# Places of matmul operands within 128-byte blocks of the on-chip memory, in a two-block hybrid layer

## The chip, the cores and the metric

The kernel runs on one core of a Trainium2 chip. The metric is the device time of one execution in microseconds (us). It is taken several times, and the median counts.

## The reference

Two model blocks run one after the other on 256 tokens of width 1024, all in float32. The first is a modulated RMS norm, a mixer of three small attentions with gates, and a convolution FFN; the second is gated linear attention, then dilated window attention. Cut to the large products:

```python
h = _rmsnorm(x, g0) * (1.0 + sc1) + sh1
z = h @ w_in                                   # 1024 -> 2248 + 3 * 1024
merged = sum(sigmoid(zg[i] + b[i]) * (y[i] @ w_branch[i]) for i in range(3))
x = x + g1 * _rmsnorm(merged @ w_out, g)
h = _rmsnorm(x, g2) * (1.0 + sc2) + sh2
a, g = split(h @ w_up, 2)                      # 1024 -> 2 * 2816
x = x + g2 * _rmsnorm((gelu(conv3(a)) * g) @ w_down, g3)
# second block: y = gla_mixer(x);  x = layer_norm(alpha * x + y)
#               y = dilated_mixer(x, shared_kv(x));  x = layer_norm(alpha * x + y)
```

## The kernel before, in words

Each float32 operand of a large product is split into a high part, rounded to the float32r type, and a low part, the remainder, in the same type. A product then takes three matmuls (`mm3`, L267): low part of the standing operand against the high part of the moving one, high against low, high against high. The class `Stream` (L100) brings the weights in one after the other: a DMA of 1 MB into a tile `raw`, then for each 1024 columns a copy on ScalarE to the tile `whi` (L154) and a subtraction on VectorE to the tile `wlo` (L155). There are six buffers of each.

The large products come in two forms. In `wstat` (L512, called by `wpair`) a 128 x 128 piece of the weights is loaded into TensorE and stands still there, while 256 columns (the tokens) of the transposed activations move through. In `tokmm` the activations are loaded 128 x 128 at a time, and 512 columns of the weights move. Every matmul has its own load, which runs while the matmul before it moves its columns. The keys of the weights of the first form are `in1`, `inc`, `zg`, `br`, `up`, `gla`, `gk`, `kvk` and `sq`; the others (`out`, `dn`, `gvg`, `gout`, `kvv`, `sout`) move.

The transposed activations of a stage are a pair of tiles (high, low) made by `big8` (L393), which use two buffers in turn: `hhi`, `hlo` for the first projections and the gates; `mhi`, `mlo` for the merged branches; `h2hi`, `h2lo` for the FFN; `x2hi`, `x2lo` for gated linear attention; `x3hi`, `x3lo` for window attention. `yhi`, `ylo` are the outputs of the three attentions.

The class `Lines` (L203) rounds every tile in the pools up to a multiple of 128 bytes, so each operand of the large products begins on a multiple of 128 bytes in each partition. A column of weights in a slice is 4 bytes, a loaded slice 512 bytes, and a moved slice 1024 or 2048 bytes.

Of the kernel before, what the change touches and what calls it, by code (L numbers as in the profile page):

```python
# [8 lines left out]
F32 = mybir.dt.float32  # L9
F32R = mybir.dt.float32r  # L10
# [8 lines left out]
S = 256  # L19
D = 1024  # L20
KK = 8
# [9 lines left out]
ORD3 = "u00 u01 c0 w00 w01 r0 n00 n01 u10 u11 c1 w10 w11 r1 N10 N11"  # L31
ORD4 = "u00 u01 c0 w00 w01 r0 u10 o00 u11 c1 o01 w10 r1 w11 o10 o11"
SC_SWA = float(128.0 ** -0.5)

COLS = {}

# [63 lines left out]
class Stream:  # L100
# [31 lines left out]
    def _chunk(self, i):  # L132
        nc = self.nc
        key, ap, n, part = self.items[i]
        if part < 0:
            raw = self.early.tile([128, n], F32, tag="early", name="early", bufs=3)
        else:
            raw = self._raw()
        if not part:
            for o in range(0, n, 1024):  # L140
                nc.sync.dma_start(raw[:, o:o + 1024], ap[:, o:o + 1024])
            self.done.append(raw)
            return
        nc.sync.dma_start(raw[:, :n], ap)
        parts = []
        for o in range(0, n, part) if part > 0 else range(0, -part, 1024):
            m = min(part, n - o) if part > 0 else min(1024, -part - o)
            hi = self.pool.tile([128, 1024], F32R, tag="whi", name="whi", bufs=self.hlbufs)
            lo = self.pool.tile([128, 1024], F32R, tag="wlo", name="wlo", bufs=self.hlbufs)
            with ExitStack() as st:  # L150
                for ins in self.behind:
                    st.enter_context(self.tc.issue_after(ins))
                st.enter_context(self.tc.high_priority(self.pri))
                i0 = nc.scalar.activation(hi[:, :m], raw[:, o:o + m], AF.Copy)  # L154
                i1 = nc.vector.tensor_sub(lo[:, :m], raw[:, o:o + m], hi[:, :m].bitcast(F32))  # L155
                self.last = (i0.ins, i1.ins)
            parts.append((hi, lo))
        self.done.append((part, parts) if part > 0 else (raw, (1024, parts)))
# [68 lines left out]
def hybrid_blocks(ctx, tc, A, out, dbg=None):  # L227
# [3 lines left out]
    cn = Lines(ctx.enter_context(tc.tile_pool(name="cn", bufs=1)), sm)  # L231
# [3 lines left out]
    def open_pool(name):  # L235
        st = ExitStack()
        p = st.enter_context(tc.tile_pool(name=name, bufs=1))
        return Lines(p, st.enter_context(tc.tile_pool(name=name + "s", bufs=1))), st.close

    p1a, close_p1a = open_pool("p1a")  # L240
    p0, close_p0 = open_pool("p0")
# [5 lines left out]
    def mm_t():  # L247
        return ps.tile([128, 512], F32, tag="mm", name="mm", bufs=2)
# [4 lines left out]
    def dump(name, t):  # L253
        if dbg and name in dbg:
            nc.gpsimd.dma_start(dbg[name], t)

    def mm(o, l, r, start, stop, share=False):
        return pe.matmul(o, l, r, start=start, stop=stop, skip_group_check=share)  # L258
# [126 lines left out]
    for h in range(4):  # L385
        sq = p0.tile([128, 2, S], F32, name="sq0", tag="sq0", bufs=2)
# [3 lines left out]
        for b in range(2):  # L390
            mm(pr[:, 256 + b:257 + b], ssq[:, b * 128:(b + 1) * 128], ones[:, 0:1], h == 0 and b == 0, h == 3, True)

    def big8(dt, name):  # L393
        return cn.tile([128, KK, S], dt, name=name, tag="big8r", bufs=2)

    hT = (big8(F32R, "hhi"), big8(F32R, "hlo"))
    qk = [acc_t(), acc_t()]
    vps = [mm_t(), mm_t()]
# [83 lines left out]
    pr = at_t()  # L482
    for b in range(2):
        mm(pr[:, b * 128:(b + 1) * 128], r1[:, b:b + 1].to_broadcast([128, 128]), ident, True, True)
    rbc = cn.tile([128, S], F32, name="rbc")
    dve.tensor_copy(rbc, pr[:, 0:S])
    h32, at = first_h(0, ga)
    for j in range(KK):
# [28 lines left out]
    def wpair(key, a, fresh=False):  # L517


        w = ws.get(key)  # L520
        p = mm_t()
        if fresh:
            for n in range(2):
                o = p[:, n * 256:(n + 1) * 256]
                W = [wsl(w, n * 1024 + k * 128, n * 1024 + (k + 1) * 128) for k in range(KK)]
                for k, l in enumerate(W):
                    mm(o, l[1], a[0][:, k, :], k == 0, False)
                    mm(o, l[0], a[0][:, k, :], False, False)
                for k, l in enumerate(W):
                    mm(o, l[0], a[1][:, k, :], False, k == KK - 1)  # L530
            return p
        for n in range(2):
            wstat(p[:, n * 256:(n + 1) * 256], w, n * 1024, a)
        return p
# [29 lines left out]
    p = wpair(("inc", 0), hT)  # L564
# [206 lines left out]
    for i in range(2):  # L771
        w = ws.get(("br", i))
        for u in range(4):
            n = 4 * i + u
            p = mm_t()
# [6 lines left out]
        if i:  # L782
            w2 = ws.get(("br", 2))
            branch2(0)
            branch2(1)
        gates(9 + 2 * i)
    mT = (big8(F32R, "mhi"), big8(F32R, "mlo"))
    for i in range(4):
        if i > 1:
# [118 lines left out]

    rms_residual(y, xn, mod[0], x1, ORD1, (xr, mod[2]))
    dump("x1", x1)  # L910
    h2 = (big8(F32R, "h2hi"), big8(F32R, "h2lo"))

    def ev_h2(j, p, act, dve):
        for low in range(2):
# [76 lines left out]
    for i in range(4):  # L991
        p = wpair(("gk", i), x2T)
        if i < 2:
            act.activation(qT[:, 2 * i:2 * i + 2, :], p, AF.Copy, scale=SC_SWA)
        else:
# [190 lines left out]
    xqt = p3.tile([128, 2, D], F32, name="lnw", tag="sg")  # L1186
    layer_norm(x2, y3, row("lng0"), None, x3, lambda i: (xkt, xqt)[i // 2][:, i % 2, :], ORD3)
    dump("x3", x3)
    x3T = (big8(F32R, "x3hi"), big8(F32R, "x3lo"))

    def ev_x3(j, p, act, dve):
        for low in range(2):
# [25 lines left out]
    for i in range(3):  # L1218
        p = wpair(("kvk", i), x3T, i == 0)
# [12 lines left out]
    sq, sgls, pTs = {}, {}, {}  # L1232
# [15 lines left out]
    def swa_scores(h):  # L1248
# [3 lines left out]
        for b in range(2):  # L1252
# [7 lines left out]
            dve.tensor_tensor_reduce(P, pl, swam[:, b, :], 1.0, -3e38, OP.add, OP.max, accum_out=st[:, 0:1])  # L1260
            dve.tensor_scalar(st[:, 1:2], st[:, 0:1], -SC_SWA, None, op0=OP.mult)
            act.activation(P, P, AF.Exp, scale=SC_SWA, bias=st[:, 1:2], accum_out=st[:, 2:3])
            dve.reciprocal(st[:, 3:4], st[:, 2:3])
# [175 lines left out]
```

## Time and profile before

| | |
|---|---|
| median of 3 runs | 743.57 us (742.25 to 746.67) |
| the profiled execution's own time | 743.82 us |
| its span, from first to last instruction | 741.8 us |
| TensorE, matmuls | busy 711.8 us, 96% |
| VectorE | busy 547.3 us, 74% |
| ScalarE | busy 407.8 us, 55% |
| mean granted clock of TensorE | 0.979 |

Matmuls overlap in such a record: a duration holds the way through the array too, so what one matmul costs in a row of them is the step from one start to the next, and not its duration. PE is TensorE's matmuls, PEld its weight loads, DVE is VectorE, ACT is ScalarE, POOL is GpSimd.

### The profile page before, as it was taken

The page shows a single profiled execution, that of the slowest core. Times are in us where ns is not written, and L with a number is a line of the kernel's source. Part 1 is how long each engine was busy: PE and PEld are TensorE (multiplying, and loading weights), DVE is VectorE, ACT ScalarE, POOL GpSimd, SP SyncE. Part 2 cuts the span into 40 slices and gives each one's busy share as a digit, 9 for nine tenths or more (in the row PEclk, how much of TensorE's full clock was granted, in tenths as well). Part 3 has the DMA queues.
Part 4 walks back from the last instruction along what each step waited for, and adds up shares of the span by engine and source line. Part 5 has one row for each costly group of instructions (what it writes and reads, how often), then busy time and mean ns, then how long its engine had stood idle before and what let it go on. Part 6 is the DMA issues. An engine that isn't in the chain of part 4 may idle for free. (4 is left out here: it accounts for less than half of the span.)

```text
span 741.8 us, 12192 instructions
## 1 busy us (share of the span) xinstructions
PE 711.8 (96%) x4878; PEld 649.1 (88%) x4878; DVE 547.3 (74%) x933; ACT 407.8 (55%) x675; POOL 20.2 (3%) x34
## 2 busy tenths in 40 slices
PE   4999999999979999999999999999989999999995
PEld 4888888998869999998999797888879999999984
DVE  5877969898868676758655756675877679677866
ACT  3447788546548455554454685343555556555542
POOL 0001000000010000000000200001010000000000
PEclk8999999999998999999999999999999999999999
DMA  8995767567634764658545454331447755433201
GB/s 313 421 350 204 291 255 296 204 240 274 243 142 171 266 246 171 243 204 307 211 179 191 142 220 171 115 114 57 166 160 253 259 189 180 158 128 131 97 1 57
DMA packets 24600, 148.74 MB, mean 201 GB/s; under 512 B 2992, under 2 KB 3248, under 8 KB 9568
## 3 DMA queue, kind: packets, MB, share of 16 engines
q1 hardware_dynamic: 21888, 139.05, 51.1%
q0 software_dynamic: 1280, 5.18, 2.1%
q10 hardware_dynamic: 1376, 3.74, 1.5%
q8 instruction: 38, 0.62, 0.3%
q14 instruction: 18, 0.15, 0.1%
HBM read 145.86 MB, written 2.10 MB: 199 GB/s over the span
## 5 line engine op out<-in xcount | busy, mean ns | idle before, releaser
L155 DVE TENSOR_TENSOR wlo<-raw,whi 128x1024 fp32r<-128x1024 f32 (+1 forms) x193 | 231.4, 1210 | 67.7 <-ACT whi L154 67.6
L154 ACT ACTIVATE whi<-raw 128x1024 fp32r<-128x1024 f32 (+1 forms) x193 | 199.4, 1050 | 95.8 <-PE acc L258 41.7
L258 PE MATMUL mm<-h2hi,wlo 128*128 128x256 f32 x352 | 100.2, 286 | 0.0
L258 PE MATMUL mm<-h2hi,whi 128*128 128x256 f32 x352 | 100.0, 285 | 0.0
L258 PE MATMUL mm<-h2lo,whi 128*128 128x256 f32 x352 | 97.3, 283 | 0.0
L258 PE MATMUL mm<-x3hi,wlo 128*128 128x256 f32 x304 | 87.9, 290 | 0.0
L258 PE MATMUL mm<-x3hi,whi 128*128 128x256 f32 x304 | 87.0, 287 | 0.0
L258 PE MATMUL mm<-x3lo,whi 128*128 128x256 f32 x304 | 83.7, 283 | 0.0
L258 PEld LDWEIGHTS mm<-h2hi,wlo 128*128 128x128 f32 x352 | 68.5, 194 | 0.3
L258 PEld LDWEIGHTS mm<-h2hi,whi 128*128 128x128 f32 x352 | 68.4, 194 | 0.0
L258 PEld LDWEIGHTS mm<-h2lo,whi 128*128 128x128 f32 x352 | 66.5, 192 | 0.4
L258 PE MATMUL mm<-hhi,wlo 128*128 128x256 f32 x208 | 60.9, 293 | 0.0
L258 PE MATMUL mm<-hhi,whi 128*128 128x256 f32 x208 | 60.4, 291 | 0.0
L258 PE MATMUL mm<-hlo,whi 128*128 128x256 f32 x208 | 60.1, 289 | 0.0
L258 PEld LDWEIGHTS mm<-x3hi,wlo 128*128 128x128 f32 x304 | 59.2, 195 | 0.2
L258 PEld LDWEIGHTS mm<-x3hi,whi 128*128 128x128 f32 x304 | 59.2, 195 | 0.0
L258 PEld LDWEIGHTS mm<-x3lo,whi 128*128 128x128 f32 x304 | 57.4, 192 | 0.0
L258 PEld LDWEIGHTS mm<-hhi,wlo 128*128 128x128 f32 x208 | 40.6, 195 | 1.8 <-issue 0.9
L258 PEld LDWEIGHTS mm<-hlo,whi 128*128 128x128 f32 x208 | 40.6, 195 | 0.8 <-issue 0.8
L258 PEld LDWEIGHTS mm<-hhi,whi 128*128 128x128 f32 x208 | 40.5, 195 | 0.6 <-issue 0.5
L440 DVE SCALAR_TENSOR_TENSOR adacc<-raw,cact,adacc 128x1024 f32<-128x1024 f32 x28 | 35.7, 1275 | 0.2
L258 PE MATMUL acc<-whi,flo 128*128 128x512 f32 x88 | 34.8, 395 | 0.0
(355 smaller groups left out, 1609.8 us busy)
## 6 DMA issues: line engine op xcount, KB each, us to landing
raw<-in_w_up_dram SPq DMA_DIRECT2D x22, 1024.0 KB, 4.8
raw<-in_w_ada_dram SPq DMA_DIRECT2D x16, 1024.0 KB, 4.8
raw<-in_swa_q_dram SPq DMA_DIRECT2D x16, 1024.0 KB, 4.9
raw<-in_w_zg_dram SPq DMA_DIRECT2D x12, 1024.0 KB, 5.2
raw<-in_w_dn_dram SPq DMA_DIRECT2D x11, 1024.0 KB, 4.8
raw<-in_w_ada_dram SPq DMA_DIRECT2D x16, 512.0 KB, 8.6
early<-in_w_in_dram SPq DMA_DIRECT2D x8, 1024.0 KB, 7.5
raw<-in_gla_vg_dram SPq DMA_DIRECT2D x8, 1024.0 KB, 4.9
```

The costliest lines, as they stand in the source:

```text
L154: i0 = nc.scalar.activation(hi[:, :m], raw[:, o:o + m], AF.Copy)
L155: i1 = nc.vector.tensor_sub(lo[:, :m], raw[:, o:o + m], hi[:, :m].bitcast(F32))
L258: return pe.matmul(o, l, r, start=start, stop=stop, skip_group_check=share)
L440: dve.scalar_tensor_tensor(a, w, c, a, op0=OP.mult, op1=OP.add)
```

## The change

The low part of a weight chunk gets a tile of 1056 columns in place of 1024. For the keys in `STILL` the low part lies 16 columns (64 bytes) into it, for the others at its start. `big8` gets 32 more columns and a parameter `past`: `h2lo` begins 64 bytes into its tile, `x3hi` 32 bytes and `x3lo` 96 bytes; `hhi`, `hlo`, `mhi`, `mlo`, `x2hi`, `x2lo` and `h2hi` begin at their tile's start as before. The tile `rbc` (1 KB) goes from the pool that lives through the program to the one of the first stage, which makes room. A `wlo` tile has 4224 bytes now, 33 times 128, so the six buffers still begin on multiples of 128.

```diff
+STILL = ("in1", "inc", "zg", "br", "up", "gla", "gk", "kvk", "sq")
...
             hi = self.pool.tile([128, 1024], F32R, tag="whi", name="whi", bufs=self.hlbufs)
-            lo = self.pool.tile([128, 1024], F32R, tag="wlo", name="wlo", bufs=self.hlbufs)
+            lo = self.pool.tile([128, 1056], F32R, tag="wlo", name="wlo", bufs=self.hlbufs)
+            lo = lo[:, 16:1040] if key[0] in STILL else lo[:, 0:1024]
...
-    def big8(dt, name):
-        return cn.tile([128, KK, S], dt, name=name, tag="big8r", bufs=2)
+    def big8(dt, name, past=0):
+        t = cn.tile([128, KK * S + 32], dt, name=name, tag="big8r", bufs=2)
+        return t[:, past:past + KK * S].rearrange("p (k s) -> p k s", k=KK)
...
-    rbc = cn.tile([128, S], F32, name="rbc")
+    rbc = p0.tile([128, S], F32, name="rbc")
...
-    h2 = (big8(F32R, "h2hi"), big8(F32R, "h2lo"))
+    h2 = (big8(F32R, "h2hi"), big8(F32R, "h2lo", 16))
...
-    x3T = (big8(F32R, "x3hi"), big8(F32R, "x3lo"))
+    x3T = (big8(F32R, "x3hi", 8), big8(F32R, "x3lo", 24))
```

No instruction is added, removed or moved by it: on each of the five engines the list of instructions, with the semaphores that each waits on, is the same before and after but for line numbers. Only addresses differ.

## Rows read from the trace of the kernel before

**Rows 1.** The page's head, busy time, and granted clock in 40 slices.
```profile
span 741.8 us, 12192 instructions
PE 711.8 (96%) x4878; PEld 649.1 (88%) x4878; DVE 547.3 (74%) x933; ACT 407.8 (55%) x675; POOL 20.2 (3%) x34
...
PEclk8999999999998999999999999999999999999999
```

**Rows 2.** Busy time by stage: stretch, length, engines (count), clock, DMA.
```profile
20.00:72.00 52.00, 52.00 (x355) 44.97 (x355) 40.41 (x73) 27.32 (x43) 1.96 (x4) 0.99 0.84 320
...
225.00:414.00 189.00, 189.00 (x1326) 177.38 (x1324) 130.24 (x176) 98.98 (x142) 1.66 (x3) 1.00 0.59 215
...
603.00:728.00 125.00, 124.97 (x939) 119.38 (x938) 94.52 (x186) 69.36 (x117) 0.00 (x0) 1.00 0.32 114
```

**Rows 3.** Groups of matmuls by shape: output<-moving,standing operand, count, busy, mean.
```profile
L258 PE MATMUL mm<-h2hi,wlo 128*128 128x256 f32 x352 | 100.2, 286 | 0.0
...
L258 PE MATMUL mm<-x3hi,wlo 128*128 128x256 f32 x304 | 87.9, 290 | 0.0
...
L258 PE MATMUL mm<-hhi,wlo 128*128 128x256 f32 x208 | 60.9, 293 | 0.0
...
L258 PE MATMUL acc<-hhi,wlo 128*128 128x256 f32 x64 | 21.7, 339 | 0.0
...
L258 PE MATMUL mm<-x2hi,wlo 128*128 128x256 f32 x72 | 21.0, 292 | 0.0
...
L258 PE MATMUL mm<-yhi,wlo 128*128 128x256 f32 x48 | 13.6, 284 | 0.0
...
L258 PE MATMUL at<-hhi,wlo 128*128 128x256 f32 x32 | 9.1, 283 | 0.0
```

**Rows 4.** Timeline of PE, FFN, 256 columns: start, duration; first and last of 13.
```profile
308.38 0.28 PE L258 MATMUL mm<-h2lo,whi 128*128 128x256 f32 x1
...
309.82 0.28 PE L258 MATMUL mm<-h2lo,whi 128*128 128x256 f32 x1
```

**Rows 5.** Timeline of PE, FFN, 512 columns: first of 15, and the next after them.
```profile
295.14 0.39 PE L258 MATMUL acc<-whi,flo 128*128 128x512 f32 x1
...
298.54 0.28 PE L258 MATMUL mm<-h2hi,wlo 128*128 128x256 f32 x1
```

**Rows 6.** Weight loads (PEld) by group: count, busy, mean of one in ns.
```profile
L258 PEld LDWEIGHTS mm<-h2lo,whi 128*128 128x128 f32 x352 | 66.5, 192 | 0.4
...
L258 PEld LDWEIGHTS acc<-whi,flo 128*128 128x128 f32 x88 | 16.6, 188 | 3.4 <-issue 0.2
```

**Rows 7.** Timeline of PE behind a short break: first and last of 5.
```profile
175.07 0.28 PE L258 MATMUL mm<-hhi,whi 128*128 128x256 f32 x1
...
175.54 0.28 PE L258 MATMUL mm<-hhi,wlo 128*128 128x256 f32 x1
```

**Rows 8.** The chain that ended last: twelve plain float32 matmuls of window attention.
```profile
603.50 1.76 PE at L258 x12
```

**Rows 9.** Timeline of PE, FFN, where 256 columns go over to 512.
```profile
327.04 0.40 PE L258 MATMUL acc<-whi,flo 128*128 128x512 f32 x1
327.27 0.40 PE L258 MATMUL acc<-wlo,fhi 128*128 128x512 f32 x1
327.51 0.39 PE L258 MATMUL acc<-whi,fhi 128*128 128x512 f32 x1
...
328.42 0.39 PE L258 MATMUL acc<-whi,flo 128*128 128x512 f32 x1
```

**Rows 10.** VectorE's split of the weights, full chunks: count, busy, mean, idle before.
```profile
L155 DVE TENSOR_TENSOR wlo<-raw,whi 128x1024 fp32r<-128x1024 f32 x185 | 223.8, 1221 | 67.4 <-ACT whi L154 67.4
```

## The prediction

> **What bounds the kernel now.** I first read the page's head: TensorE's matmuls fill 96% of the span, VectorE 74% and ScalarE 55%, and the granted clock stands at its upper level (2.4 GHz) in nearly every slice [rows 1]. Since a busy share is an average, I then read busy time by stage [rows 2]. In the FFN (225 to 414 us) TensorE is busy for all 189.0 us at clock 1.00, beside 130.2 us of VectorE and a DMA share of 0.59. In window attention (603 to 728 us) it is busy for 125.0 of 125 us, beside 94.5 us of VectorE. So what matters there is how long TensorE takes for each matmul. The first stage (20 to 72 us) is different: TensorE counts as busy too, but the DMA engines run at 0.84 and 320 GB/s, so weights arriving late may set its pace.
>
> The change moves addresses alone. The question is therefore how much of a matmul's step depends on where its operands lie. The timeline gives the step. In the FFN, 12 steps of 256-column matmuls take 309.82 - 308.38 = 1.44 us, 120.0 ns each [rows 4]; 15 steps with 512 columns take 298.54 - 295.14 = 3.40 us, 226.7 ns each [rows 5]. The difference is 106.7 ns for 256 columns, 0.417 ns a column, one cycle at 2.4 GHz. So both lengths carry the same fixed part, 120.0 - 106.7 = 13.3 ns. This part is what a change of place could make smaller or larger, because the columns themselves already go through at a cycle each.
>
> Three readings say that it is not wholly a constant. Behind a short break the same matmuls at the same addresses take 175.54 - 175.07 = 0.47 us for four steps, 117.5 ns each [rows 7]: 2.5 ns less, only because loads and moving columns meet at another moment. Where 256 columns go over to 512, the first two steps take 327.51 - 327.04 = 0.47 us, 235 ns each, 8.3 ns more than the settled 226.7, and the first six 230 [rows 9]. And a weight load takes 192 ns as a rule beside the 256-column stream but 188 beside the 512-column one [rows 6]. So the weights read and the moving columns read appear to get in each other's way, by an amount that depends on how they are placed against each other in time. All operands of these products begin on multiples of 128 bytes, so the two streams always meet in the same way; another place is a shift that the trace of before never shows.
>
> **The change, part by part.** While a matmul moves its columns, the weights of the next one are loaded. In `mm3` the high activations move beside a load of the high weights, then the low activations beside the high weights, then the high activations beside the next low weights. I count those meetings in which the two addresses differ modulo 128 after the change, and before did not.
>
> - *`wlo` 64 bytes on.* It shifts one meeting in three: 208 + 64 + 32 = 304 for the first projections and gates, 72 for `x2`, 48 for `y` [rows 3]. Together 424.
> - *`h2lo` 64 bytes on.* With `wlo`, two of three meetings in the FFN's first product are shifted by 64: 2 x 352 = 704 [rows 3].
> - *`x3hi` 32 and `x3lo` 96 bytes on.* All three are shifted by 32 or 96: 3 x 304 = 912 [rows 3]. The 96 matmuls of `kvv`, where `x3` stands still, are shifted as well, but are few, and I leave them out.
>
> That is 424 + 704 + 912 = 2,040 matmuls. The price of one is not in the trace, so I bound it. *Gain:* the twelve rows of [rows 8] are plain float32 (six matmuls, each recorded as two rows) and move 2,048 columns in 1.76 us, 0.86 ns a column, about two cycles each. Two cycles a column would be 1.707 us, so at most (1.76 - 1.707)/12 = 4.4 ns remain as a fixed part. If the 13.3 ns fell to that, a shifted matmul would gain 8.9 ns: 2,040 x 8.9 = 18.2 us. *Loss:* if a shifted matmul ran like the first two of [rows 9], it would lose 8.3 ns: 16.9 us. *Between:* the 2.5 ns of [rows 7] would give 5.1 us. I take a gain of 4.5 ns, nearer to the last since it is the same instruction at the same addresses, only met otherwise; the plain float32 type is a further row. 2,040 x 4.5 = 9.2 us. Of it, the 64 + 32 meetings of the first stage may be covered by late weights (96 x 4.5 = 0.4 us), which leaves 8.8 us.
>
> *Costed at nothing:* the rest. VectorE's subtraction writes a `wlo` 64 bytes on; a full chunk takes 1,221 ns and VectorE stood idle for 67.4 us ahead of these, waiting for ScalarE [rows 10]. If each of the 185 took 5% longer (61 ns), that would be 11.3 us over a span in which VectorE is idle for 194 us [rows 1], so TensorE would have to catch up with it first. In the FFN it could shorten by a fifth before the 130.2 us of VectorE came near [rows 2]. `rbc` is one tile of the first stage. No DMA, wait or queue changes.
>
> The Trainium skill's page SBUF — State Buffer (section A bandwidth-pool intuition that's wrong) speaks against this: it gives TensorE a second, independent read port for weight loads beside that of the moving operand, and says that contention comes only from a port lock or a starved descriptor generator, not from sharing. By that rule the fixed 13.3 ns is not contention, and the sum is zero; by [rows 6, 7, 9], in which the step and the load both vary without a change of operand, it is not zero. The rows show no address at work, though, so the rule becomes a rival below.
>
> **The sum.** 743.8 (the profiled execution's own time, 2.0 us over its span, 0.25 over the median) - 8.8 = 735.0 us; against the median 734.8. I say 735.
>
> **The rivals.**
> - *Places do nothing.* The variation in [rows 7, 9] is one of moments alone, and soon settles again to 13.3 ns whatever the addresses. The time stays at 743.6. For it: 13.3 ns is the same for both lengths, as a plain constant would be. Against it: the steps that fall below it.
> - *Shifted operands cost more.* A 512-byte slice that begins 64 bytes past a multiple of 128 touches five blocks of 128 bytes instead of four, and a moved 1,024 bytes nine instead of eight. If such a block is what is read at a time, each shifted meeting pays. At the 230 ns of the first six steps in [rows 9] that is 3.3 ns: 2,040 x 3.3 = 6.7 us, 750.5; at the bound of 8.3 ns it is 760.7. It decides from 1.8 ns a matmul on (3.7 us, 0.5%). For it: a meeting in another phase did go slower. Against it: that was for a few matmuls only, and the stream settled again.
> - *The fixed part falls to that of plain float32.* 743.8 - 18.2 = 725.6. For it: [rows 8]. Against it: [rows 7] shows no stretch of several matmuls below 117.5.
> - *TensorE gains, another engine does not follow.* With VectorE at 130.2 of 189.0 us I give this no share of its own.
>
> **How the numbers follow.** Some gain, as summed: 0.50, between 726 and 740. The whole fixed part: 0.11. Nothing: 0.23. Costs more: 0.16. A measurement here tells about 0.5% (3.7 us) from no change. The partial gain would be under that if the price were below 1.8 ns, which I give a tenth of its chance, so faster is 0.45 + 0.11 = 0.56, the same 0.23 + 0.05 = 0.28, slower 0.16. For 8 in 10, the range reaches up past "nothing" to the middle of the slower case and down to near the whole gain: 725 to 749.
>
> **What would show it.** The step in window attention, all meetings shifted, should fall from 120 to about 115.5 ns; in the FFN's first product two steps in three; among the gates one in three. The loads of 192 ns should come to 188 or less. The 512-column steps of `dn` should stay at 226.7, since their operands keep their places modulo 128. VectorE's 1,221 ns should stay. I would be wrong if 256-column steps stayed at 120.0 everywhere, or settled above it, or if the two offsets (64 and 32) acted in opposite directions, so that one stage gained and another lost.

## The result

The changed kernel takes 736.44 us (median of 4 runs, 733.62 to 739.09) against 745.12 us (median of 4, 742.25 to 749.20) for the kernel before, run beside it. The ratio is 0.9897, with a 95% interval from 0.9863 to 0.9932: 1.0% faster, 5 to 10 us. 735 was predicted, in a range of 725 to 749.

In the profiled execution the span went from 741.8 to 731.6 us, and the matmuls' busy time by 11.2 us, against [rows 1]. The two profiled executions differ in mean granted clock too (0.979 before, 0.986 after), so the medians tell more than this pair. The page's head after the change:

```profile
span 731.6 us, 12192 instructions
PE 700.6 (96%) x4878; PEld 636.4 (87%) x4878; DVE 547.1 (75%) x933; ACT 407.1 (56%) x675; POOL 20.2 (3%) x34
```

The busy times of VectorE and ScalarE did not change by more than 0.7 us; TensorE's steps are what became shorter. The timeline of the FFN after the change (start, duration, instruction; 16 matmuls in a row, of which the first and the last stand here):

```profile
299.08 0.28 PE L262 MATMUL mm<-h2hi,whi 128*128 128x256 f32 x1
...
300.81 0.28 PE L262 MATMUL mm<-h2hi,whi 128*128 128x256 f32 x1
```

15 steps take 1.73 us, 115.3 ns each, where [rows 4] had 120.0. The chain that ended last shows window attention (start, length, instructions):

```profile
594.30 1.75 PE at L262 x12
...
610.03 5.67 PE mm L262 x48
```

The pair of weights at the same place of the chain before:

```profile
619.39 5.75 PE mm L258 x48
```

The twelve rows of plain float32 matmuls, whose operands the change does not name, take 1.75 us, beside 1.76 in [rows 8]. The 48 matmuls of one weight pair take 5.67 us, 118.1 ns each, beside 5.75 us, 119.8 each, before. The weight loads of the FFN (count, busy, mean of one) came from 192 ns [rows 6] to 188:

```profile
L262 PEld LDWEIGHTS mm<-h2lo,whi 128*128 128x128 f32 x352 | 65.1, 188 | 0.3
```

VectorE's split of the weights stayed as it was in [rows 10], and its idle time ahead of it shrank a little:

```profile
L159 DVE TENSOR_TENSOR wlo<-raw,whi 128x1024 fp32r<-128x1024 f32 x185 | 223.7, 1221 | 62.9 <-ACT whi L158 62.9
```

One part went the other way. In the projection of the merged branches, where 512 columns of weights move, 14 steps after the change take 194.71 - 191.43 = 3.28 us, 234 ns each, and the same 14 before took 197.86 - 194.66 = 3.20 us, 229 each. After, then before:

```profile
191.43 0.40 PE L262 MATMUL acc<-whi,mhi 128*128 128x512 f32 x1
...
194.71 0.40 PE L262 MATMUL acc<-wlo,mhi 128*128 128x512 f32 x1
```

```profile
194.66 0.40 PE L258 MATMUL acc<-whi,mhi 128*128 128x512 f32 x1
...
197.86 0.39 PE L258 MATMUL acc<-wlo,mhi 128*128 128x512 f32 x1
```

Single steps are too short for the views' hundredths of a microsecond, so I worked the means out of the start times in each trace: from the start of one float32r matmul to the start of the next, leaving out steps over 135 ns (256 columns) and over 245 ns (512), which hold a wait. They are reproducible: the FFN's three steps (high activations beside a load of high weights, low beside high, high beside low), with the same places in three different kernels (the change, e8, e12), came out at 113.7, 118.2, 115.3, then 113.9, 118.3, 115.5 and 113.9, 118.3, 115.4. All kernels, in ns (`gates, first` are the first projections and the gates):

```
                  gates,   FFN    gated    window   branches  512 columns
                  first           lin. at. att.               (weights move)
before            119.8    119.9   120.0   119.8   120.0      228.1
the change        116.6    115.7   117.8   117.9   117.8      230.0
e1_tiles_only     118.0    117.9   118.9   117.9   119.4      230.2
e2_lo_only        116.3    116.1   117.8   116.3   117.7      230.0
e3_acts_only      118.0    118.1   118.4   117.8   119.4      230.1
e4_lo64_all       117.9    118.0   117.8   117.8   117.0      231.6
e5_grid_low64     116.9    117.8   117.9   117.7   117.7      231.8
e6_grid_low128    119.1    117.7   119.1   118.4   119.2      232.7
e7_grid_low0      115.7    118.0   119.9   117.7   119.8      228.4
e8_no_x3          116.5    115.9   117.9   116.7   117.7      230.0
e9_acts64         116.4    117.8   119.9   116.9   119.6      228.2
e10_grid_even     116.9    120.1   117.8   115.5   119.9      229.2
e11_acts192       114.3    117.2   119.9   116.1   119.3      227.6
e12_x3_as_ffn     116.8    115.9   117.8   116.3   117.8      229.8
matmuls           912      1,056   216     912     144        792
```

From the first two lines the time adds up: gates 912 x 3.2 ns = 2.9 us, FFN 1,056 x 4.2 = 4.4, window attention 912 x 1.9 = 1.7, gated linear attention 216 x 2.2 = 0.5, branches 144 x 2.2 = 0.3; together 9.8 us gained, and 792 x 1.9 = 1.5 lost at 512 columns. Net 8.3 us, beside 8.7 between the medians. That is closer than this sum can be trusted: for the other kernels that ran several times it is off by up to 3 us (e3 4.2 beside 4.2 us, e4 3.7 beside 1.5, e8 9.3 beside 11.8, e11 11.8 beside 8.9).

The mean granted clock of the profiled executions lay between 0.976 and 0.993 with no relation to the places, which may be one reason why the times of two runs of one kernel differ by more than some of the effects below. Of the 47 runs of the kernel before that stand beside the experiments, the 24 with a mean granted clock under 0.984 have a mean time of 744.6 us, and the 15 from 0.989 on 743.2. The steps tell more than the times.

### The profile page after: what moved, and what is told of

It is laid out like the page before. It is cut to its first block, busy times and chain, and to the rows that moved or that the text cites. A ratio compares the mean times of both kernels' runs of the same rounds, so it can differ in the third digit from the quotient of the medians.

```text
span 731.6 us, 12192 instructions
## 1 busy us (share of the span) xinstructions
PE 700.6 (96%) x4878; PEld 636.4 (87%) x4878; DVE 547.1 (75%) x933; ACT 407.1 (56%) x675; POOL 20.2 (3%) x34
## 5 line engine op out<-in xcount | busy, mean ns | idle before, releaser
L262 PE MATMUL mm<-h2hi,wlo 128*128 128x256 f32 x352 | 98.3, 280 | 0.0
L262 PE MATMUL mm<-h2hi,whi 128*128 128x256 f32 x352 | 98.1, 280 | 0.0
L262 PE MATMUL mm<-x3hi,wlo 128*128 128x256 f32 x304 | 86.2, 285 | 0.0
L262 PE MATMUL mm<-x3hi,whi 128*128 128x256 f32 x304 | 85.1, 281 | 0.0
L262 PEld LDWEIGHTS mm<-h2hi,wlo 128*128 128x128 f32 x352 | 67.0, 190 | 0.4
L262 PEld LDWEIGHTS mm<-h2hi,whi 128*128 128x128 f32 x352 | 66.9, 190 | 0.0
L262 PE MATMUL mm<-hhi,whi 128*128 128x256 f32 x208 | 58.7, 282 | 0.0
L262 PEld LDWEIGHTS mm<-x3hi,wlo 128*128 128x128 f32 x304 | 57.7, 190 | 0.0
L262 PEld LDWEIGHTS mm<-x3hi,whi 128*128 128x128 f32 x304 | 57.5, 189 | 0.0
L262 PEld LDWEIGHTS mm<-hhi,wlo 128*128 128x128 f32 x208 | 39.0, 188 | 2.5 <-PE mm L262 0.8
```

## The experiments

Three theories were at stake at first. *Meetings* (the prediction's): a step depends on the distance, modulo 128, of the moving columns and the weights loaded meanwhile, each step for itself. *The row*: 120 ns is what a row of matmuls settles at when all its meetings are alike, and one odd operand keeps the whole row from it. *The tiles*: it is not the 64 bytes but the larger tiles, which put the buffers at other multiples of 128.

**e1, the tiles alone.**

```diff
-            lo = lo[:, 16:1040] if key[0] in STILL else lo[:, 0:1024]
+            lo = lo[:, 0:1024]
-    h2 = (big8(F32R, "h2hi"), big8(F32R, "h2lo", 16))
+    h2 = (big8(F32R, "h2hi"), big8(F32R, "h2lo"))
-    x3T = (big8(F32R, "x3hi", 8), big8(F32R, "x3lo", 24))
+    x3T = (big8(F32R, "x3hi"), big8(F32R, "x3lo"))
```

> The larger tiles of the change, but every operand at its tile's start, so all places are multiples of 128 bytes again and only their distances modulo 512 differ from before (the six low-part buffers step by 4,224 bytes). If the 64 and 32 bytes are what works, 256-column steps settle at 120.0 ns as before and the time is that of before, 743 to 747 us. If the steps came down because the buffers no longer lie alike modulo 512, they stay at 113 to 118 ns and the time at 735 to 738. The 512-column steps of the merged branches, which went from 227 to 232 ns with the change though their operands stayed on multiples of 128, tell the same by themselves: 227 by the first theory, 232 by the second.

Measured: 738.07 us against 743.53, ratio 0.9942 (0.9920 to 0.9965). All operands lie on multiples of 128 bytes, and yet the steps came down to about 118 and the 512-column steps rose to 230.2, as with the change. So multiples of 128 are not all alike. In this run the step in which `hhi` moves beside a load of `wlo` was 117.3 to 117.5 ns at distances of 0 and 256 bytes and 119.1 to 119.2 at 128 and 384: places count modulo 256 at least. Neither of the two outcomes that I had named came out in full.

**e2, only the low weights; e3, only the activations.** e2 keeps the change's line for `lo` and drops the places of `h2lo`, `x3hi` and `x3lo`; e3 does the reverse.

> Only the low parts of the standing weights lie 64 bytes on; all activations begin on multiples of 128. My prediction's count by meetings: only the step in which high activations meet the load of the next low weights changes, to about 115, the two others stay at 120; gain 3 to 4 us. The rival, that one odd operand keeps the whole row of steps from settling: all three steps change in every stage, to a mean of 116 to 117 per triple as among the gates after the change; gain about 1,080 triples x 10 ns = 10.8 us, as much as the whole change, so 734 to 737 us.

> Low weights on multiples of 128, activations as in the change (h2lo 64, x3hi 32 and x3lo 96 bytes on). By meetings: in the FFN one step in three changes (low activations beside high weights), in window attention all three as in the change; gates and first projections stay at 120; gain 352 x 4.5 + 912 x 2 ns = 3.4 us. By the rival (one odd operand unsettles the row): FFN and window attention as after the change (triples of 347 and 354 ns), gates at 360 as before; gain about 352 x 13 + 304 x 6 ns = 6.4 us, 738 us.

Measured: e2 735.14 us, 0.9894 (0.9869 to 0.9919), the whole gain of the change. e3 739.34 us, 0.9946 (0.9930 to 0.9962), no more than the tiles alone. In e2's gates the step with no new distance modulo 256 (high activations beside high weights) fell to 114.5, the shifted one (beside low weights) to 114.0, and the third, with `hlo` 128 bytes off because of its larger tile, stayed at 120.4; in e1 the first and the third, at the same distances, had 116.9 and 118.8. So a step is not set by its own meeting alone, and the theory of meetings falls in this form.

**e4, 64 bytes without the tiles.** Low weights come from a pool of their own behind a gap of 64 bytes, with tiles of the old size, so the high weights and the large activations keep their distance modulo 512. The two gaps together put the pools opened behind them (`y` and the operands that stand still in most 512-column products) 128 bytes on.

```diff
+    gp1 = ctx.enter_context(tc.tile_pool(name="gp1", bufs=1))
+    gt1 = gp1.tile([128, 16], F32, name="gt1")
+    nc.gpsimd.memset(gt1, 0.0)
+    wl = Lines(ctx.enter_context(tc.tile_pool(name="wl", bufs=1)))
...
-            lo = self.pool.tile([128, 1056], F32R, tag="wlo", name="wlo", bufs=self.hlbufs)
-            lo = lo[:, 16:1040] if key[0] in STILL else lo[:, 0:1024]
+            lo = self.wl.tile([128, 1024], F32R, tag="wlo", name="wlo", bufs=self.hlbufs)
```

> All low weights, those that move too, 64 bytes past a multiple of 128, with tiles of the old size, so that high and low buffers keep their distance modulo 512; all activations on multiples. If 64 bytes is what works and distances modulo 512 are not, 256-column steps come out as in the run with the low parts alone (116 to 117 ns on average), and the 512-column steps show what a moved operand at 64 bytes does: 227 if nothing, 230 to 235 if it unsettles these too. If distances modulo 512 do it, 120 ns.

Measured: 742.01 us, 0.9985 (0.9966 to 1.0005). The 64 bytes alone bring 256-column steps to 117.9, no further than the tiles alone do, and 512-column steps rise to 231.6, also in the projection of the merged branches (from 227 to 232), where of the operands only the low weights were shifted. Between e1, e4 and e2, the 64 bytes and the tiles' 128 bytes each give about 2 ns a step, and both together 3.4 (means over all five stages).

**e5 to e7, grids.** Buffers alike modulo 256 (`big8` with 64 more columns, pools with gaps), and another place of the activations in each stage. The edit of e7:

```diff
-    hT = (big8(F32R, "hhi"), big8(F32R, "hlo"))
+    hT = (big8(F32R, "hhi", 16), big8(F32R, "hlo", 16))
-    x3T = (big8(F32R, "x3hi", 8), big8(F32R, "x3lo", 24))
+    x3T = (big8(F32R, "x3hi", 0), big8(F32R, "x3lo", 32))
```

> Tiles padded so that all buffers lie alike modulo 256; places in bytes: high weights 0, low weights 64 in every stage; activations (high, low): first projections and gates (0, 128), FFN (0, 64), window attention (64, 64). Read by steps, three per triple, in the order of the meetings high-high weights, low-high weights, high-low weights. By meetings of their own (each step set by the distance of its two addresses): gates 120/less/less, FFN 120/less/less, window attention less/less/120. By the row that does not settle: none of the nine at 120; the gates come out near 348 ns a triple as in the run with the low parts alone, since it has the same distances modulo 256, the FFN near 347 as after the change, window attention near 354 as in the run with all low parts at 64.

> As the grid before, with low weights at 128 bytes; activations: gates (0, 0), FFN (0, 128), window attention (0, 64). If only places modulo 128 count, gates and FFN stay at 120.0 and window attention alone comes down. If places modulo 256 count, as the tiles alone suggest (steps of 119.3 at distances of 128 and 384 and 117.5 at 0 and 256), gates and FFN come down to about 118 too, and window attention, with 64 and 128 in play, to 116.

> As the grids before, with low weights at 0; activations: gates (64, 64), FFN (0, 64), window attention (0, 128). The gates are the case that parts the theories: every meeting is 64 bytes apart, and all three alike. By meetings of their own the step leaves 120 everywhere (113 to 118). By the row that settles whenever its three meetings are alike, it stays at 120.0 (360 a triple). FFN: by meetings 120/less/120; by the row all three near 118. Window attention as the FFN.

Each was run once (744.39, 743.64 and 740.54 us, beside a median of 745.50), so only the steps are read. e7 gives the control: gated linear attention and the branches, with all operands at 0 modulo 256, stay at 119.9 and 119.8, and the 512-column steps at 228.4. Its gates, with all meetings alike but 64 bytes apart, fell to 115.7, so a row does not settle at 120 whenever its meetings are alike, and the theory of the row falls too, though e7's FFN had all three steps near 118, as that theory said. In e6 the gates with the low weights 128 bytes off have 119.1 and no longer a steady 120.0, and window attention 118.4, where 116 was expected. e5 gave its gates 116.9 (expected 116.0 to 116.3), its FFN 117.8, where 115.7 was expected, and window attention 117.7 as expected.

**e8, the change without the places of window attention.** The line of `x3T` as in e1, all else as changed.

> The change without the places of window attention: x3hi and x3lo at their tile's start, all else as changed. Its triple was 353.8 ns after the change and 348.4 in the run with the low parts alone. If those 32 and 96 bytes cost, the time falls by 304 x 5.4 ns = 1.6 us against the change, to about 734.8, and the triple comes to 348; if they help, it rises and the triple stays at 354 or above.

Measured: 733.71 us against 745.50, 0.9860 (0.9826 to 0.9894). The triple (three successive steps) fell from 353.8 to 350.0 ns, less than the 348 expected, but in that direction: the 32 and 96 bytes cost about 1.2 ns a step, 912 x 1.2 = 1.1 us. The interval of the time overlaps with that of the change, so only the steps show it.

**e9 and e10, one distance for a whole stage.** e9 as e7, with `past` 16 for both parts of `hT`, `h2` and `x3T`; e10 with 8, 24 and 48 for these, and 16 for `x2T`.

> All weights, high and low, still or moved, at the same place modulo 256; the activations that move past standing weights (gates, FFN, window attention) all 64 bytes on, high and low. Every meeting there is 64 bytes apart. If the distance of the two addresses is what counts, all three stages have 115.8 ns a step (347 a triple) as the gates in the grid with low weights at 0, the 512-column steps stay at 227 to 228.5, the first of gated linear attention and the branches at 120.0, and the time is 10 to 13 us under before: 0.983 to 0.987 of it. If it needs a difference between the loads, the FFN and window attention stay at 120.

> As the run before, with one distance for all meetings of a stage: 32 bytes in the first projections and gates, 96 in the FFN, 192 in window attention, 64 in gated linear attention. If the cost depends on the distance alone, each stage has one step of its own, alike for its three meetings: by symmetry 192 as 64 (115.8), and 32 and 96 between that and the 120.0 of 0, about 117 to 119. If 64-byte halves are what counts, 32 stays near 120 and 96 comes to 116. Gated linear attention comes from 120 to 116; its 512-column steps, where activations 64 bytes on stand still and weights move, show whether these leave 228.

Measured: e9 738.60 us against 744.75, 0.9910 (0.9877 to 0.9944). The 512-column steps stayed at 228.2, as expected, and all three stages left 120, but they did not agree: 116.4, 117.8, 116.9. The chain shows why. Three weight pairs of window attention in e9:

```profile
610.76 5.66 PE mm L263 x48
...
618.17 5.45 PE mm L263 x48
...
624.49 5.65 PE mm L263 x48
```

The same 48 matmuls with the same distances take 5.66 or 5.45 us: 117.9 ns a step or 113.5, and nothing between. In the start times, the long ones repeat 118, 117, 118, the short ones 113, 113, 114. So at 64 bytes a row settles in one of two steady rhythms, and it keeps that one to its end, while its weights come from several buffers in turn. Of all groups of three steps in e9, 32% among the gates, none in the FFN and 21% in window attention lie at the lower one.

How a row begins has a part in the choice. The first projections and the gates are placed alike in e7 and e9, and yet had 115.7 and 116.4 ns. One row of the first stage, in e7 and then in e9 (the matmul ahead, the row's first matmul, and the one nine steps on):

```profile
44.50 0.68 PE L263 MATMUL acc<-hhi,wlo 128*128 128x256 f32 x1
45.02 0.28 PE L263 MATMUL acc<-hlo,whi 128*128 128x256 f32 x1
...
46.04 0.28 PE L263 MATMUL acc<-hlo,whi 128*128 128x256 f32 x1
```

```profile
43.40 0.59 PE L263 MATMUL acc<-hhi,wlo 128*128 128x256 f32 x1
43.82 0.28 PE L263 MATMUL acc<-hlo,whi 128*128 128x256 f32 x1
...
44.88 0.28 PE L263 MATMUL acc<-hlo,whi 128*128 128x256 f32 x1
```

Begun 0.52 us behind the matmul ahead, it runs at 113.3 ns a step; begun 0.42 us behind it, at 117.8. All seven such rows of the first stage begin after 0.52 us in e7 and run at 113.3; of the same seven in e9, the two that begin after 0.42 and 0.38 us run at 117.8, and the five after 0.52 or 0.32 us at 113.3. Further along, in window attention, the order returns (5.66, 5.45, 5.66 us), with the same work ahead of each. In e10 (735.60 us in one run, beside 744.75), 192 bytes gave window attention 115.5, 32 gave the gates 116.9, and 96 left the FFN at 120.1, with steps of up to 125; 64 gave gated linear attention 117.8, and cost its 512-column steps 5 ns (228 to 233), since there the same activations stand still. The expected symmetry of 64 and 192 was there in the two rhythms, but not in the means: 115.5 at 192 is a mixture of 113.3 and 117.8.

**e11, 192 bytes in all three stages; e12, window attention placed as the FFN is.** e11 is e9 with `past` 48; e12 is the change with `x3T` at 0 and 16.

> As the run with activations 64 bytes on, with 192 bytes instead, in all three stages. If the distance alone sets the step, all three stages come to the 115.5 ns that window attention had at 192 in the grid (346.6 a triple), 512-column steps stay at 227 to 229, and the time is 960 triples x 13.2 ns = 12.7 us under before, 0.983 of it. If the step also hangs on how the row before it ended, the three stages differ from each other by a nanosecond or more, as they did at 64 (116.4, 117.8, 116.9).

> The change with window attention placed as the FFN is: x3hi at its tile's start, x3lo 64 bytes on. If places set the step, its triple comes from 353.8 ns to the FFN's 347.2 and the time falls by 304 x 6.6 ns = 2.0 us against the change, to 0.986 to 0.987 of before. If the stage has a step of its own whatever the places, the triple stays at 350 or more.

Measured: e11 734.51 us against 743.41, 0.9881 (0.9849 to 0.9913). The stages differ as at 64 bytes: 114.3, 117.2, 116.1, by how many of their rows settle low (78%, 13% and 39% of the groups of three steps). The chain of e11:

```profile
604.54 5.46 PE mm L263 x48
...
611.75 5.46 PE mm L263 x48
...
618.08 5.66 PE mm L263 x48
```

and a stretch of its timeline in the low rhythm, 12 of 12 steps in 607.90 to 609.26 us, 113.3 ns each:

```profile
607.90 0.28 PE L263 MATMUL mm<-x3lo,whi 128*128 128x256 f32 x1
...
609.26 0.28 PE L263 MATMUL mm<-x3lo,whi 128*128 128x256 f32 x1
```

e12: 735.55 us, 0.9886 (0.9853 to 0.9920). Its window attention has 114.5, 118.4, 116.0 ns for the three steps of a triple, beside 113.9, 118.3, 115.4 in its FFN: the places carry their steps from one stage to another, to 0.6 ns. e2, e8, e11 and e12 lie between 0.986 and 0.990 of before, as the change does at 0.9897, and these runs don't tell them apart; there is no clear winner over the change.

## Why the prediction came out, and where it did not

**That TensorE sets the pace, and that a shorter step is a shorter time:** right. The steps account for 8.3 us of 8.7 (within the 3 us of such sums), and VectorE's split stayed at 1,221 ns.

**That the fixed 13.3 ns is no constant:** right, and it is what the forecast rested on. With all operands alike it is 13.3 (control in e7); the steady rhythms of e9 and e11 leave 117.8 - 106.7 = 11.1 and 113.3 - 106.7 = 6.6. The rival in which places do nothing is refuted, by e1 as much as by the change. The Trainium skill's page SBUF — State Buffer (section A bandwidth-pool intuition that's wrong) gives TensorE a second, independent read port for weight loads and puts contention down to structure, not to shared bandwidth. Here the step settles between 113.3 and 120.0 ns by the operands' addresses and by how a row begins, so the sum of zero that the prediction drew from that page did not come. Whether it is the two reads that get in each other's way, and through what, no run here shows.

**The step that failed: "I count those meetings in which the two addresses differ modulo 128 after the change, and before did not", 2,040 at 4.5 ns.** Three things were wrong in it. Meetings that were not counted gained: among the gates after the change, high activations beside high weights fell to 114.9 and beside the shifted low weights to 114.4, while low activations beside high weights stayed at 120.2. Where every meeting was shifted, in window attention, the gain was the smallest, 1.9 ns a step. And modulo 128 was too coarse, since the larger tiles by themselves do about half of it (e1). What was measured in its place is all 3,240 steps at 3.0 ns on average, 9.8 us. That 735 came out so near is luck: more steps gained, each gained less, and 1.5 us were lost where nothing was expected.

**The parts of the sum.** First projections and gates, FFN and window attention were put at 304, 704 and 912 meetings of 4.5 ns: 1.4, 3.2 and 4.1 us (`x2` and `y` 0.5 together; the 0.4 us taken off for late weights no run here tests by itself). They measured 2.9, 4.4 and 1.7 (0.8 for the two). Steps of a stage should have fallen in the order window attention, FFN, gates; they fell in the order FFN, gates, window attention.

**That 512-column steps would stay at 226.7:** wrong. "Since their operands keep their places modulo 128" is the same mistake. They rose by 1.9 ns on average, 1.5 us, because the low weights' buffers now step by 33 x 128 bytes; with these alike modulo 256 they are back at 227.6 to 228.4 (e7, e9, e11).

**The rival that costs more** did not come as a whole, but its direction exists: 512-column steps in every kernel whose low weights lie off a multiple of 256, and the FFN with its activations 96 bytes on, which lost the whole gain.

**The rival in which the fixed part falls to that of plain float32** did not come. The nearest was 6.6 ns, half of it, in some of the rows (78% of the groups of three among the gates of e11). If every 256-column step took 113.3 ns, the time would by estimate be 3,240 x 6.5 = 21 us under before, which no kernel here reached.

**Open:** how the moment at which a row begins picks the rhythm, and how to bring every row into the lower one; the waits ahead of a row were not varied on purpose. Open too is whether the distance of the two operands counts, as the text says for short, or the place of each by itself. The high weights lie on a multiple of 256 bytes in every kernel here, and no run moves all operands by the same 64 bytes, which would part the two.

## What to carry to other kernels

Read the step from start to start, not the busy time, and where it stands at the same number for thousands of matmuls, look at what of it is not columns. Laying all operands alike is not the best: here operands on multiples of 256 bytes locked TensorE's 256-column float32r matmuls at 120.0 ns, and moving the activations or the low weights by 64 bytes brought the stages to means of 116 to 118; but moving the low weights slowed the matmuls with 512 moving columns (231.6 ns in e4 beside 228.1), so it has to be tried for each form. A larger tile that is meant as room for an offset is a change of place too, for every buffer behind it, and has to be tested by itself.

## What the hardware showed that I had not expected

- Rows of float32r matmuls have steady rhythms. 256 columns settle at 120.0, 117.8 or 113.3 ns a step, by the operands' addresses and by how the row begins (at the same places 113.3 after 0.52 us and 117.8 after 0.42, e7 and e9); with mixed distances the FFN of the changed kernel settles on a repeating triple of about 113, 118 and 115, while its window attention wanders between 114 and 124 and does not settle.
- Buffers at different multiples of 128 bytes are not alike. 117.3 to 117.5 ns at distances of 0 and 256 bytes, 119.1 to 119.2 at 128 and 384 (e1).
- 64 and 192 bytes give the same two rhythms in different shares: of the groups of three steps in the first projections and gates, 32% (e9) and 48% (e7) lie at 113.3 ns with 64 bytes, 78% (e11) with 192.
